# Putting parts of the split weights 64 bytes further on in SBUF, so that the starts of a matmul's moving operand and of the next matmul's weights fall in chosen halves of 128 bytes

## The chip, the cores and the metric

The kernel runs on one core of a Trainium2 chip. The metric is the device time of one launch in microseconds (us); the table below gives three runs of the kernel before.

## The reference

A four-part encoder trunk over 256 tokens of width 1024, in float32: a layer with neighbourhood attention and latent attention side by side, an MLP, a layer of dilated attention, a second MLP, and RMS norms between them. Cut to the parts whose weights the change touches:

```python
def sq_relu_mlp(xn, w1, w2):
    return jnp.square(jax.nn.relu(xn @ w1)) @ w2

def odd_mixer(xn, w_in, w_o, cos_f, sin_f):
    b, s, _ = xn.shape
    hcat = (xn @ w_in).reshape(b, s, DIL_GROUPS, 3, DIL_HEADS, HEAD_DIM)
    q = apply_rope(hcat[:, :, :, 0], cos_f, sin_f)
    k = apply_rope(hcat[:, :, :, 1], cos_f, sin_f)
    v = hcat[:, :, :, 2]
    return dilated_attention(q, k, v) @ w_o

for layer in range(DEPTH):                     # DEPTH = 2
    xn = rms_norm(x, norm_mix[layer])
    ...                                        # even_mixer, then odd_mixer
    x = x + sq_relu_mlp(rms_norm(x, norm_mlp[layer]), mlp_w1[layer], mlp_w2[layer])
return rms_norm(x, norm_final)
```

## The kernel before, in words

**Split operands.** Every product is made of float32r matmuls on operands that are split in two: a high part (`hi`, a cast on ScalarE, line 201) and a low part (`lo`, the difference, on VectorE, line 202). Most products take three matmuls (`mm3`, lines 205 to 207): high weights by high, high by low, low by high. Two products pack the first two into one of 512 columns, because high and low parts of the activations lie side by side in the tile `pair` (`[P, 8, 2, 256]`): the MLP's up projection (line 391: high weights by 512 columns of `pair`; line 394: low weights by its 256 high columns) and the odd layer's queries and keys (lines 911 and 914, the same way).

**Weights.** They come from HBM in blocks of up to 2048 columns into four `raw` buffers (`load_weight`, line 163) and are split in four pieces each (`split_piece`, line 178) into the tiles `whi` and `wlo` of the pool `wsp`, three buffers each, one block ahead of use (`weight`, line 192). The list `specs` (lines 131 to 158) fixes the order of the blocks. The very first blocks are split by hand in the even layer (lines 593 to 628), where `views` (line 594) makes the tiles.

**Which operand is which.** A matmul has a stationary operand, loaded by an instruction of its own (LDWEIGHTS, on the profile's PEld), and a moving one that streams past it. TensorE's weight load for the next matmul runs while the present one streams. The block's weights are stationary in the up projections (`w1`), the odd layer's queries and keys (`w_oqk`), and the even layer's queries and keys and both output projections. They are the moving operand, with the activations stationary, in the values (`w_v` of the even layer, `w_ov` of the odd one: 512 columns, stationary `pair`), the latent parts, and the down projections (`w2`: 512 columns, stationary `hh` and `hl`).

**Order.** In an MLP, each step makes the next 256 features (32 matmuls of lines 391 and 394) and folds in the features of three steps before (24 matmuls of lines 205 to 207). In the odd layer the blocks of `w_oqk` and `w_ov` are woven with the attention of the unit before (`ODD_PLAN`, `weave`).

**Where the tiles lie.** In the program as built (byte addresses within a partition): `pair` begins at 26944, which is 64 past a multiple of 128, in the second half of 128 bytes. The three `whi` begin at 121216, 129408 and 137600 and the three `wlo` at 145792, 153984 and 162176, all at multiples of 128 (and 384 past a multiple of 2048), in the first half. `hh` and `hl` also begin in the first half, the mixed heads `oah`, `oal`, `obh` and `obl` in the second. Nearly every slice that a matmul takes starts a multiple of 128 bytes into its tile, so the half of the tile is the half of the operand.

Of the kernel before, what the change touches and what calls it, by code (L numbers as in the profile page):

```python
# [17 lines left out]
F32R = mybir.dt.float32r  # L18
# [5 lines left out]
P = 128  # L24
# [10 lines left out]
WCH = 2048  # L35
# [3 lines left out]
SPLIT_AHEAD = 2  # L39
WPARTS = 4  # L40
NORM_PRIO = 300

QK_ORDER = (0, 2, 1)


def odd_weights():


    v = lambda b, c: [("w_ov", b, c, h) for h in range(2)]
    qk = lambda u, js=QK_ORDER: [("w_oqk", u, j) for j in js]  # L50
    out = [p for pair in zip(v(0, 0), v(0, 1)) for p in pair] + qk(0)
    for step in ODD_PLAN:
        for kind, *at in step:
            out += v(*at) if kind == "v" else qk(*at)
    return out
# [13 lines left out]
def trunk(ctx, tc, a, out):  # L69
# [6 lines left out]
    wsp = ctx.enter_context(tc.tile_pool(name="wsp", bufs=WBUFS))  # L76
    ps = ctx.enter_context(tc.tile_pool(name="ps", bufs=4, space=PSUM))

    def scratch(shape, name):

        n = int(np.prod(shape))
        v = work.tile([P, 512], F32, tag="scratch", name=name, bufs=12)[:, :n]
        if len(shape) == 2:
            v = v.rearrange("p (a b) -> p a b", b=shape[1])
        return v
# [45 lines left out]
    specs = []  # L131

    def plan(name, n):
        for j in range(a[name].shape[0]):
            specs.append((a[name][j], n))

    def plan_mlp(layer):
        for j in (0, 1):
            specs.append((a["w1"][layer, j], WCH))
        for j in range(2, 16):  # L140
            specs.append((a["w1"][layer, j], WCH))
            specs.append((a["w2"][layer, j - 2], WCH))
        for j in (14, 15):
            specs.append((a["w2"][layer, j], WCH))

    CV = 416 + 512
    plan("w_cv", 2 * CV)
# [5 lines left out]
    plan("w_oe", 2 * D)  # L153
    plan_mlp(0)
    for kind, *at in odd_weights():
        specs.append((a[kind][tuple(at)], WCH))
    plan("w_oo", 2 * D)
    plan_mlp(1)

    parts = {}  # L160
    state = {"loaded": 0, "split": 0, "used": 0}

    def load_weight(edges=None, earlier=lambda i: None):
        j = state["loaded"]
        src, n = specs[j]
        raw = wraw.tile([P, WCH], F32, tag="raw", name="raw")
        edges = edges or (0, n)
        for i, c in enumerate(slice(*e) for e in zip(edges, edges[1:])):
            earlier(i)
            nc.sync.dma_start(raw[:, c], src[:, c])  # L170
        parts[j] = [raw, None, None]
        state["loaded"] = j + 1

    def cut(j, i, n):
        w = specs[j][1] // n
        return slice(i * w, (i + 1) * w)

    def split_piece(eng=None):
        j, i = divmod(state["split"], WPARTS)
        if i == 0:  # L180
            parts[j][1:] = (wsp.tile([P, WCH], F32R, tag=n, name=n) for n in ("whi", "wlo"))
        raw, hi, lo = (z[:, cut(j, i, WPARTS)] for z in parts[j])
        state["split"] += 1
        return split(hi, lo, raw, eng)
# [15 lines left out]
    def split(hi, lo, src, eng=None):  # L200
        a = nc.scalar.copy(hi, src).ins  # L201
        return a, (eng or nc.vector).tensor_tensor(lo, src, hi.bitcast(F32), op=ALU.subtract).ins  # L202
# [35 lines left out]
    def prepare(k, n, xT):  # L238

        hi, lo, gk = xT[0][:, k, :], xT[1][:, k, :], gains[:, n * KT + k:n * KT + k + 1]  # L240
        return (lambda: nc.scalar.activation(hi, x[:, k, :], AF.Copy, scale=gk),
                lambda: nc.vector.scalar_tensor_tensor(lo, x[:, k, :], gk, hi.bitcast(F32), ALU.mult, ALU.subtract))  # L242
# [21 lines left out]
    def rstd(s):  # L264

        r = work.tile([P, NT], F32, tag="rstd", name="rstd")
        nc.gpsimd.tensor_tensor(r, columns(s), mhalf.broadcast_to([P, NT]), op=ALU.pow)
        return r
# [19 lines left out]
    def column(r, t):  # L288
        return r[:, t:t + 1]
# [8 lines left out]
    def join(b, o, n, xT):  # L298

        v = x[:, 2 * b:2 * b + 2, :]  # L300
        nc.vector.tensor_tensor(v, two(o), v, op=ALU.add)
        for f in zip(*(prepare(k, n, xT) for k in (2 * b, 2 * b + 1))):
            run_all(f)

    def hand_over(accs, last, n):

        xT, s = pair_tile(), sum_tile()
        for b in range(4):
            last[b]()
            with tc.high_priority(NORM_PRIO):  # L310
                join(b, accs[b], n, xT)
        return xT, s

    def hand_over_tokens(accs, last, n, scale):
# [4 lines left out]
        def leave(h, t):  # L319
            last(h, t)  # L320
            acc, sc = accs[2 * t + h], column(scale, t)
            with tc.high_priority(NORM_PRIO):
                y = ys[h, t] = scratch([512], "y")
# [3 lines left out]
        def turn(h):  # L327
            with tc.high_priority(NORM_PRIO):
                for b in range(2):
                    pt = bank("w")  # L330
                    for k in range(2):
                        for t in range(NT):
                            c = (2 * b + k) * P
                            nc.tensor.transpose(pt[:, k * T + t * P:k * T + (t + 1) * P], ys[h, t][:, c:c + P], ident)
                    join(2 * h + b, pt, n, xT)
# [181 lines left out]
    def even(ep):  # L517
# [36 lines left out]
        def product(o, n, w, k, t, passes=range(3)):  # L554

            xs = xh[:, k, tok(t)], xl[:, k, tok(t)], xh[:, k, tok(t)]
            for i in passes:
                nc.tensor.matmul(o[:, 0:n], xs[i], (w[1], w[1], w[2])[i], start=(k, i) == (0, 0), stop=(k, i) == (KT - 1, 2))  # L558
# [26 lines left out]
        def v_out(t, pv):  # L585
            nc.scalar.activation(vna[:, t, :], pv, AF.Copy, scale=column(r, t))
# [6 lines left out]
        with tc.manual_schedule(engines={ENG.PE, ENG.Activation, ENG.DVE}):  # L593
            def views(j, c0, c1):
                if parts[j][1] is None:
                    parts[j][1:] = (wsp.tile([P, WCH], F32R, tag=n, name=n) for n in ("whi", "wlo"))
                return [z[:, c0:c1] for z in parts[j]]

            for k in range(KT):
                upper, lower = prepare(k, 0, xT)  # L600
                upper()
                if k < 4:
                    c0 = k % 2 * CV
                    wc, wv = views(k // 2, c0, c0 + 416), views(k // 2, c0 + 416, c0 + CV)
                else:
                    wc, wv = views(2, (k - 4) * 416, (k - 3) * 416), None
                if k == 0:

                    nc.vector.tensor_copy(wc[1], wc[0])
                    lower()  # L610
                    nc.vector.tensor_tensor(wc[2], wc[0], wc[1].bitcast(F32), op=ALU.subtract)
                else:
                    lower()
                    split(wc[1], wc[2], wc[0])
                if wv:
                    split(wv[1], wv[2], wv[0])

                if k in (3, 5, 6, 7):
                    squares.pop(0)()
                for w, ps_, n in ((wc, pc, 416), (wv, pv, 512)):  # L620
                    if w is not None:
                        for passes in ((0,), (1,), (2,)) if k == 0 else (range(3),):
                            for t in range(NT):
                                product(ps_[t], n, w, k, t, passes)
            state["split"] = 3 * WPARTS
            for i in range(2 * WPARTS):
                split_piece()
            wv = [z.rearrange("p (k n) -> p k n", k=4) for z in parts[3]]
            for t in range(NT):
                for k in range(4, KT):  # L630
                    product(pv[t], 512, [z[:, k - 4] for z in wv], k, t)
                    if (t, k) == (0, 5):
                        r = rstd(s)
            rs = work.tile([P, 2, NT], F32, tag="rs", name="rs", bufs=1)
            for i, n in enumerate((256, 128)):
                nc.vector.tensor_scalar(rs[:, i, :], r, n ** -0.5, None, ALU.mult)
            dg = [diagonal(r, t) for t in range(NT)]
            turn_c = [c_tail(t, pc[t]) for t in range(NT)]
            state["used"] = 4
            for j in range(4):  # L640
                del parts[j]
            for t in range(NT):
                v_out(t, pv[t])
# [176 lines left out]
        at = -5  # L820
# [11 lines left out]
    def odd(op, xT, s):  # L832
# [22 lines left out]

        def value_steps(b, c, prio=NORM_PRIO, tag="acc"):

# [39 lines left out]
        def qk_steps(d, js=QK_ORDER):  # L897
# [4 lines left out]
            def gemm(b, f, half):  # L902
# [12 lines left out]
                if half == 1:  # L915
                    with tc.high_priority(NORM_PRIO):
                        if f == 0:
# [48 lines left out]
        def attention(u, d):  # L966
# [36 lines left out]
            def mix(out_tag):  # L1003
                pvo = bank(out_tag)
                v0, v12 = values_of(u)
                for i in range(NT):
# [4 lines left out]
                    for c in range(2):  # L1011
                        qs = slice(64 * c, 64 * c + 64)
                        for j in range(2):
                            cs = slice(64 * j, 64 * j + 64)
                            nc.tensor.matmul(pvo[cs, i * P + 64 * c:i * P + 64 * c + 64], v12[:, 2 * i + c, cs], turned[i, j][:, 2, qs], start=False, stop=c == 1)
                with tc.high_priority(NORM_PRIO):
                    split(*(z[:, u % 4, :] for z in mixed[u // 4]), pvo[:, 0:T])
# [152 lines left out]
```

## Time and profile before

| what | value |
|---|---|
| median of three runs | 742.25 us (741.9 to 743.02) |
| the profiled execution's own time | 742.68 us |
| its span in the profile | 740.9 us |
| granted TensorE clock | 0.998 of full |
| PE busy | 732.5 us, 99% of the span, 4539 matmuls |
| VectorE busy | 538.6 us, 73% |
| ScalarE busy | 471.4 us, 64% |
| DMA | 180 GB/s mean |

The profile records when each matmul starts and how long it takes. Matmuls overlap: the next one starts before the one before has drained. So there are two ways to read what one costs: the distance from one start to the next (its gap), and its recorded duration, which is longer than the gap by about the same amount for all of one width. A group's row in the list of one source line gives the count and the shortest, median and longest duration in ns.

### The profile page before, as it was taken

How to read it: one execution, taken by the hardware profiler on the slowest of the kernel's cores; microseconds unless marked ns; L12 is line 12 of the kernel's file. 1: busy time of each engine (PE TensorE's matmuls, PEld its weight loads, DVE VectorE, ACT ScalarE, POOL GpSimd, SP SyncE). 2: the span in 40 equal slices, each digit the busy share in tenths (PEclk: the TensorE clock that was granted, in tenths of full speed). 3: DMA queues.
4: the chain of work that ended last, by engine and by line, in shares of the span. 5: the costliest groups of instructions: out<-in, count | busy, mean ns of one | idle time of the engine just before them, and what ended most of it. 6: DMA issues, size and time to landing. Idle time of an engine off the chain costs nothing.

```text
span 740.9 us, 11984 instructions
## 1 busy us (share of the span) xinstructions
PE 732.5 (99%) x4539; PEld 628.5 (85%) x4539; DVE 538.6 (73%) x1100; ACT 471.4 (64%) x1020; POOL 8.4 (1%) x20
## 2 busy tenths in 40 slices
PE   9999999999999999999999999999999999999996
PEld 6988998888888887888888888888898888888885
DVE  6878859766665666689968886899559765665674
ACT  7788967554455456468877668687857455455441
POOL 0100000000000001000000000000000000000000
PEclk9999999999999999999999999999999999999999
DMA  8773335565555554655664545455546555545501
GB/s 291 313 263 108 115 114 177 175 218 174 197 197 178 202 188 155 232 160 171 208 220 147 221 145 182 139 192 173 188 152 220 178 175 197 197 171 189 206 4 57
DMA packets 24585, 133.17 MB, mean 180 GB/s; under 512 B 3664, under 2 KB 4816, under 8 KB 10192
## 3 DMA queue, kind: packets, MB, share of 16 engines
q1 hardware_dynamic: 24384, 132.28, 52.0%
q8 instruction: 35, 0.57, 0.3%
q14 instruction: 22, 0.18, 0.1%
q10 hardware_dynamic: 144, 0.13, 0.1%
HBM read 127.16 MB, written 1.05 MB: 173 GB/s over the span
## 4 chain that ended last, share of the span: by engine, by line
PE 94%; DMA 1%; DVE 1%; issue 1%; ACT 1%; SPq 1%; POOLq 0%; POOL 0%
PE w L391 16%; PE acc L205 13%; PE acc L207 13%; PE acc L206 13%; PE acc L911 11%; PE w L394 8%; PE acc L914 5%; PE acc L558 2%; PE w L214 1%; PE w L999 1%; PE w L205 1%; PE w L768 1%; PE w L207 1%; PE w L206 1%; PE w L979 1%
## 5 line engine op out<-in xcount | busy, mean ns | idle before, releaser
L202 DVE TENSOR_TENSOR wlo<-raw,whi 128x512 fp32r<-128x512 f32 (+2 forms) x471 | 303.0, 679 | 68.2 <-ACT whi L201 67.6
L201 ACT CAST whi<-raw 128x512 fp32r<-128x512 f32 (+2 forms) x471 | 261.9, 614 | 140.5 <-PE acc L207 57.0
L391 PE MATMUL w<-pair,whi 128*128 128x512 f32 x512 | 125.0, 395 | 0.0
L391 PEld LDWEIGHTS w<-pair,whi 128*128 128x128 f32 x512 | 95.2, 187 | 22.9 <-DVE pair L242 0.6
L911 PE MATMUL acc<-pair,whi 128*128 128x512 f32 x384 | 101.6, 401 | 0.0
L205 PE MATMUL acc<-whi,hh 128*128 128x512 f32 x250 | 97.9, 392 | 0.0
L207 PE MATMUL acc<-whi,hl 128*128 128x512 f32 x250 | 97.7, 391 | 0.0
L206 PE MATMUL acc<-wlo,hh 128*128 128x512 f32 x250 | 97.6, 390 | 0.0
L911 PEld LDWEIGHTS acc<-pair,whi 128*128 128x128 f32 x384 | 67.7, 188 | 12.4 <-issue 0.2
L398 DVE TENSOR_TENSOR u<-w,side 128x256 f32<-128x256 f32 x64 | 26.9, 421 | 57.2 <-ACT side L397 57.1
L394 PEld LDWEIGHTS w<-pair,wlo 128*128 128x128 f32 x512 | 63.4, 188 | 2.9
L394 PE MATMUL w<-pair,wlo 128*128 128x256 f32 x512 | 63.9, 277 | 0.0
L201 ACT CAST hh<-hsq 128x512 fp32r<-128x512 f32 x32 | 19.9, 622 | 56.4 <-DVE hsq L400 56.4
L207 PEld LDWEIGHTS acc<-whi,hl 128*128 128x128 f32 x250 | 47.0, 188 | 9.7
L914 PEld LDWEIGHTS acc<-pair,wlo 128*128 128x128 f32 x384 | 51.2, 188 | 4.4
L205 PEld LDWEIGHTS acc<-whi,hh 128*128 128x128 f32 x250 | 47.0, 188 | 8.7
L206 PEld LDWEIGHTS acc<-wlo,hh 128*128 128x128 f32 x250 | 46.9, 188 | 8.8
L914 PE MATMUL acc<-pair,wlo 128*128 128x256 f32 x384 | 51.9, 278 | 0.0
L205 PE MATMUL acc<-whi,pair 128*128 128x512 f32 x80 | 32.3, 403 | 0.0
L207 PE MATMUL acc<-whi,pair 128*128 128x512 f32 x80 | 31.5, 393 | 0.0
L206 PE MATMUL acc<-wlo,pair 128*128 128x512 f32 x80 | 31.2, 390 | 0.0
L990 ACT ACTIVATE pp<-sn,dmn 128x384 f32<-128x384 f32 x32 | 19.7, 614 | 9.8 <-DVE dmn L988 8.9
(220 smaller groups left out, 1102.4 us busy)
## 6 DMA issues: line engine op xcount, KB each, us to landing
raw<-in_w SPq DMA_DIRECT2D x64, 1024.0 KB, 4.8
raw<-in_w_oqk SPq DMA_DIRECT2D x24, 1024.0 KB, 4.9
raw<-in_w_ov SPq DMA_DIRECT2D x12, 1024.0 KB, 5.0
raw<-in_w_qk SPq DMA_DIRECT2D x4, 1024.0 KB, 8.6
raw<-in_w_oe SPq DMA_DIRECT2D x4, 1024.0 KB, 5.3
sw<-qk SPq DMA_DIRECT2D x64, 64.0 KB, 2.0
raw<-in_w_oo SPq DMA_DIRECT2D x4, 1024.0 KB, 5.3
bias<-in_rpb SPq DMA_DIRECT2D x8, 256.0 KB, 4.6
```

The costliest lines, as they stand in the source:

```text
L201: a = nc.scalar.copy(hi, src).ins
L202: return a, (eng or nc.vector).tensor_tensor(lo, src, hi.bitcast(F32), op=ALU.subtract).ins
L205: nc.tensor.matmul(o, sh, mh, start=first, stop=False)
L206: nc.tensor.matmul(o, sh, ml, start=False, stop=False)
L207: nc.tensor.matmul(o, sl, mh, start=False, stop=last)
L391: nc.tensor.matmul(two(pu[f]), w[0][:, cut_of(k, f)], xT[2][:, k], start=k == 0, stop=False)
L394: nc.tensor.matmul(pu[f][:, 0:T], w[1][:, cut_of(k, f)], xT[0][:, k, :], start=False, stop=k == KT - 1)
L398: nc.vector.tensor_tensor(u[:, f], pu[f][:, 0:T], side[:, f], op=ALU.add)
L558: nc.tensor.matmul(o[:, 0:n], xs[i], (w[1], w[1], w[2])[i], start=(k, i) == (0, 0), stop=(k, i) == (KT - 1, 2))
L911: nc.tensor.matmul(two(pq), wh[:, cut_of(k)], xp[:, k], start=k == 0, stop=False)
L914: nc.tensor.matmul(pq[:, 0:T], wl[:, cut_of(k)], xh[:, k, :], start=False, stop=k == KT - 1)
L990: nc.scalar.activation(pp, sn, AF.Exp, bias=mn, scale=-1.0, accum_out=z)
```

## The change

The tiles `whi` and `wlo` grow from 2048 to 2080 columns (by 128 bytes), and of each the 2048 columns that begin either at its start or 16 columns (64 bytes) in are used. `SHIFTS` says which: the high part of `w1` and of `w_oqk` is put off by 64 bytes and the low part is not; both parts of `w_v` and `w_ov` are put off; all other weights stay at the start of their tiles.

As the tiles are longer, the later buffers also move: in the program as built the three `whi` tiles begin at 121216, 129536 and 137856 and the three `wlo` at 146176, 154496 and 162816. These are still multiples of 128, but 384, 512 and 640 (and 768, 896 and 1024) past a multiple of 2048. All other tiles keep their half of 128 bytes. The instructions of every engine, their order and their waits stay the same.

```diff
+LINE = 16
+SHIFTS = {"w1": (LINE, 0), "w_oqk": (LINE, 0), "w_ov": (LINE, LINE), "w_v": (LINE, LINE)}
+
...
     def plan(name, n):
         for j in range(a[name].shape[0]):
-            specs.append((a[name][j], n))
+            specs.append((a[name][j], n, SHIFTS.get(name, (0, 0))))
 
     def plan_mlp(layer):
         for j in (0, 1):
-            specs.append((a["w1"][layer, j], WCH))
+            specs.append((a["w1"][layer, j], WCH, SHIFTS["w1"]))
...
     for kind, *at in odd_weights():
-        specs.append((a[kind][tuple(at)], WCH))
+        specs.append((a[kind][tuple(at)], WCH, SHIFTS[kind]))
...
+    def split_tiles(j):
+        return [wsp.tile([P, WCH + 2 * LINE], F32R, tag=n, name=n)[:, o:o + WCH] for n, o in zip(("whi", "wlo"), specs[j][2])]
+
...
     def split_piece(eng=None):
         j, i = divmod(state["split"], WPARTS)
         if i == 0:
-            parts[j][1:] = (wsp.tile([P, WCH], F32R, tag=n, name=n) for n in ("whi", "wlo"))
+            parts[j][1:] = split_tiles(j)
...
             def views(j, c0, c1):
                 if parts[j][1] is None:
-                    parts[j][1:] = (wsp.tile([P, WCH], F32R, tag=n, name=n) for n in ("whi", "wlo"))
+                    parts[j][1:] = split_tiles(j)
```

More of the change, by code (lines that the diff above doesn't have):

```diff
@@ L134, in plan @@
         for j in range(a[name].shape[0]):
-            specs.append((a[name][j], n))
+            specs.append((a[name][j], n, SHIFTS.get(name, (0, 0))))
     def plan_mlp(layer):
         for j in (0, 1):
-            specs.append((a["w1"][layer, j], WCH))
+            specs.append((a["w1"][layer, j], WCH, SHIFTS["w1"]))
         for j in range(2, 16):
-            specs.append((a["w1"][layer, j], WCH))
-            specs.append((a["w2"][layer, j - 2], WCH))
+            specs.append((a["w1"][layer, j], WCH, SHIFTS["w1"]))
+            specs.append((a["w2"][layer, j - 2], WCH, (0, 0)))
         for j in (14, 15):
-            specs.append((a["w2"][layer, j], WCH))
+            specs.append((a["w2"][layer, j], WCH, (0, 0)))
     CV = 416 + 512
@@ L164, in load_weight @@
         j = state["loaded"]
-        src, n = specs[j]
+        src, n, _ = specs[j]
         raw = wraw.tile([P, WCH], F32, tag="raw", name="raw")
```

## Prediction

> **What bounds the kernel now.** I read the page first, for the engine that fills the span, and the chain of waits that ended last.
>
> ```profile
> span 740.9 us, 11984 instructions
> PE 732.5 (99%) x4539; PEld 628.5 (85%) x4539; DVE 538.6 (73%) x1100; ACT 471.4 (64%) x1020; POOL 8.4 (1%) x20
> PEclk9999999999999999999999999999999999999999
> PE 94%; DMA 1%; DVE 1%; issue 1%; ACT 1%; SPq 1%; POOLq 0%; POOL 0%
> ```
>
> PE is busy for 99% of the span, the clock is full in every slice, and 94% of the closing chain is PE. The waits of PE alone say whether anything feeds it late:
>
> ```profile
> PE acc L117 <- DVE warm L112: 1.2, 1, 1.2
> PE w L979 <- DVE q L940: 0.7, 1, 0.7
> PE acc L205 <- DVE obl L202: 0.2, 1, 0.2
> ```
>
> These three rows are all there is, 2.1 us together. So the time is a sum of gaps between matmul starts, and a matmul that starts its successor 1 ns earlier 1,000 times takes 1 us off the end. An edit that leaves instructions, order and waits alone can act only on those gaps (or on the splitting engines, below). The question is whether the gap depends on where operands begin. Next I read the list by source line of every large group of 512 columns; the three figures are shortest, median and longest duration in ns.
>
> ```profile
> L391 PE MATMUL w<-pair,whi x512: 388/394/497, 113.5 to 715.9; 128*128 128x512 f32 x171
> L911 PE MATMUL acc<-pair,whi x384: 388/394/504, 315.3 to 513.1; 128*128 128x512 f32 x192
> L205 PE MATMUL acc<-whi,hh x250: 387/389/484, 130.3 to 729.5; 128*128 128x512 f32 x125
> L206 PE MATMUL acc<-wlo,hh x250: 387/389/481, 130.5 to 729.8; 128*128 128x512 f32 x125
> L207 PE MATMUL acc<-whi,hl x250: 387/389/478, 130.8 to 730.0; 128*128 128x512 f32 x125
> L205 PE MATMUL acc<-whi,pair x80: 388/394/481, 292.1 to 525.6; 128*128 128x512 f32 x80
> L206 PE MATMUL acc<-wlo,pair x80: 388/388/398, 292.3 to 525.8; 128*128 128x512 f32 x80
> L207 PE MATMUL acc<-whi,pair x80: 391/392/400, 292.5 to 526.0; 128*128 128x512 f32 x80
> ```
>
> All are 128x128 weights by 512 columns, and yet they have two medians. Against the built program's addresses the difference has a pattern. In the down projections (hh, hl) the moving operand and the weights loaded beside it for the next matmul both begin in the first half of 128 bytes: 389. In the up projection and in the odd layer's queries and keys (L391, L911) pair moves from the second half while the next weights come from the first: 394. The values (whi or wlo moving, pair stationary) have different halves too, and lie between, 388 to 394. At 256 columns the sign turns round:
>
> ```profile
> L394 PE MATMUL w<-pair,wlo x512: 276/276/283, 117.9 to 717.8; 128*128 128x256 f32 x171
> L914 PE MATMUL acc<-pair,wlo x384: 276/276/287, 317.2 to 514.1; 128*128 128x256 f32 x192
> L205 PE MATMUL w<-whi,hh x12: 277/283/283, 730.2 to 734.2; 128*128 128x256 f32 x12
> L206 PE MATMUL w<-wlo,hh x12: 282/283/283, 730.3 to 734.3; 128*128 128x256 f32 x12
> L914 PE MATMUL acc<-pair,wlo x6: 276/276/283, 405.2 to 405.8; 128*128 128x256 f32 x6
> ```
>
> Different halves (L394, L914) take 276, the same half (hh at 256 columns, in the tail) 283. The last row is the best test that the trace has: it is the end of one run of eight, of which the last is followed by a transpose whose weights begin in pair's own half. That last one is the 283; its neighbours, with the same line, shape and moving tile, are 276. Over the span ten matmuls of L914 are followed so, and each takes 280 to 283.
>
> **What a gap is worth.** Durations end by a model, so I take the price from starts, in the timeline of one MLP step (start, length, line, operands):
>
> ```profile
> 153.06 0.39 PE L205 MATMUL acc<-whi,hh 128*128 128x512 f32 x1
> ...
> 158.51 3.89 PE L391 MATMUL w<-pair,whi 128*128 128x512 f32 x16
> 162.25 1.99 PE L394 MATMUL w<-pair,wlo 128*128 128x256 f32 x16
> ```
>
> From 153.06 to 158.51 stand 24 matmuls of the down projection: 5.45 / 24 = 227.1 ns each. From 158.51 to 162.25 stand 16 of L391: 3.74 / 16 = 233.8 ns. The starts give 6.7 ns, the medians 394 - 389 = 5; I take 6 for L391. For the odd layer the chain has runs of eight:
>
> ```profile
> 349.31 1.87 PE acc L911 x8
> 361.62 2.06 PE acc L911 x8
> 364.59 1.86 PE acc L911 x8
> ```
>
> 1.87 / 8 = 233.8 in quiet runs; 2.06 holds a stall of about 0.19 us that the halves don't touch. In the trace's starts these gaps alternate between about 231 and 236, and the first of a run is often 226, so I take 5 there.
>
> **The change part by part.** Nothing is added or removed, no DMA, queue or wait moves. The counts are of pairs (a matmul and the one behind it on PE), from the addresses of both built programs.
>
> - High part of w1, 64 bytes on: 480 of L391's 512 pairs go from different halves to the same. 480 x 6 = 2.9 us gained. The other 32 stand before L394, whose low weights stay in the first half: unchanged.
> - High part of w_oqk: 324 pairs of L911, 324 x 5 = 1.6 us.
> - Both parts of w_ov, the moving operand: 284 pairs in thirds. To 389 from 394 (L205), 388 (L206) and 392 (L207) is 5, -1 and 3, a mean of 2.3: 284 x 2.3 = 0.65 us.
> - Both parts of w_v in the even layer: 23 pairs of L558, by the same mean 0.05 us.
> - What is lost: 29 pairs of 512 columns go from same to different (24 of them the last down matmul before the next L391), 29 x 6 = 0.17 us; 38 of 256 columns go from different to same (low weights ahead of a shifted high part), 38 x 7 by the 283 and the 276 = 0.27 us.
>
> The sum is 2.9 + 1.6 + 0.65 + 0.05 - 0.17 - 0.27 = 4.8 us gained. The low products L394 and L914, 896 matmuls, keep different halves, which is the cheaper case at 256 columns; the down projections keep the same half, the cheaper one at 512.
>
> ScalarE and VectorE now write the shifted tiles from 64 bytes on. The trace has no such write of this shape, only the aligned ones:
>
> ```profile
> L202 DVE TENSOR_TENSOR wlo<-raw,whi 128x512 fp32r<-128x512 f32 x456 | 295.5, 684 | 66.6 <-ACT whi L201 66.0
> L201 ACT CAST whi<-raw 128x512 fp32r<-128x512 f32 x456 | 255.1, 618 | 138.7 <-PE acc L207 57.0 <-issue 55.5 <-PE acc L911 8.7
> 310.00:550.00 240.00, 239.18 (x1713) 208.28 (x1712) 192.39 (x393) 178.14 (x377) 0.69 (x1) 1.00 0.54 179
> ```
>
> The window of the odd layer (columns PE, PEld, VectorE, ScalarE) shows the tightest place: VectorE is busy for 192 of 240 us there. A few per cent on 684 ns would stay hidden beside PE; the faster PE leaves it 240 - 2.3 us, still 80% busy. I cost the writes at nothing. If each took a quarter longer (171 ns), a third of the 456, some 150, falling here would add 26 us, VectorE would reach 218 of 238 us and its peaks would begin to hold PE up, so this decides only from about there.
>
> On the profiled execution's footing the time is 742.68 - 4.8 = 737.9. That execution was 0.43 above the median of the runs, so against the median it is 742.25 - 4.8 = 737.4 us.
>
> **Bounds.** Taking 6.7 for all of L391 and L911 gives 5.4, and 388 for the values (6, 0, 4) 284 x 3.3 = 0.9: with the losses 5.9, so 736.4. Taking 4 for L391, 3 for L911 and nothing for the values gives 1.9 + 1.0 - 0.4 = 2.5, so 739.8. The forecast's own range is 736 to 740.
>
> **Rivals.**
>
> *The operands' starts don't matter.* The 389 and the 394 would then belong to the products: another moving tile, another PSUM tile, other work on VectorE beside them. The time would stay 742.3. For it speaks that L206 on pair has 388 with different halves. Against it speaks the 283 at the end of a run of 276, where only the next weights differ (in type too, which is its weakness), and the three hh rows at 256. The Trainium skill, in "SBUF — State Buffer", section "SBUF: two separate sides", has it that TensorE, ScalarE and VectorE's own pair of ports never wait for anyone, so that two reads by TensorE could not meet; by that rule the gain is nothing and the time 742.3. No run here has yet set it against a shifted tile; the 283 beside 276 speaks against it. Chance 0.13, with the case that the shift doesn't do what it says.
>
> *The distance matters over 256 bytes, not 128: slower.* The longer tiles put whi and wlo 128 bytes apart from each other in their place modulo 256. Now 331 pairs of the down projections go from a distance of 0 to 128, and 330, 217 and 157 of the gaining pairs of L391, L911 and the values arrive at 128 and not at 0. The trace of before has no pair of 512 columns at 128. If 128 costs c ns more than 0, the change is worth 331c + 330(c - 6) + 217(c - 5) + 157(c - 2.3) ns, with the pairs that do reach 0 worth -1.7 us and the losses 0.4 us: 1.035c - 4.8 us. It is slower from c = 4.6; with c = 6, the price that 64 has, the time is 742.25 + 1.4 = 743.7. Of the 256-column pairs 783 move from a distance of 64 to 192 as well; at up to 7 ns each they would add up to 5.5, so 749 at the worst. For it speaks that the values, at 192, cost 388 to 394 and not 394 throughout; against, that within L391 and within the down projections one value rules. I give it 0.10.
>
> *The moving operand alone decides.* A stream from the second half would be slow at 512 columns whatever the weights do. L391 and L911 stay at 394, and the values, now moving from the second half, rise from 388 to 394 to 394 throughout: 284 x 2.7 = 0.8 us, so 743.0. The values' present place between 388 and 394 speaks for it, the 283 after the 276 against. Chance 0.05.
>
> *The shifted writes slow the splits* so far that VectorE holds PE up in the odd layer, above: a time over 743. Chance 0.02.
>
> **How the numbers follow.** The forecast has 0.70, the rivals 0.13, 0.10, 0.05 and 0.02. About 0.2%, 1.5 us, is what a measurement of this kernel can tell from no change, so faster means below 740.8 and slower above 743.7. The forecast is faster in nearly all of its range, and I give 0.02 of the period rival (c well below 4.6) to it: 0.72. Same gets the first rival, most of the moving-operand one and some of the period one: 0.19. Slower gets the rest, 0.09. The range must take in the unchanged time to leave no more than 2 in 10 outside: 736.0 to 742.8.
>
> **What would show it.** In the profile after, the medians of L391 and L911 (seven lines further down) fall from 394 to about 389, with 388 to 389 for all three rows of the values; the hh rows stay at 389, and the low products at 276. If L391 has two values by buffer, or hh rises to 394 for some, the period rival is right; if 394 stays, one of the other two. The splits stay near 684 and 618. I am wrong if the gaps fall and the span doesn't, because then PE isn't what the time is made of.

## The result, and the profile after

The changed kernel takes 746.16 us (median of 6 runs, 746.04 to 746.78) against 742.28 (6 runs, 741.89 to 743.02): a ratio of 1.0052, 95% interval 1.0039 to 1.0065. It is slower by 3.9 us where 4.8 us of gain were forecast. The profiled execution took 746.22 us, 3.5 more than that of before.

The page of the changed kernel and its waits of PE say that the bound is the same: PE fills the span, and what it waits for is less than before (1.4 us, not 2.1).

```profile
span 744.4 us, 11984 instructions
PE 736.7 (99%) x4539; PEld 631.1 (85%) x4539; DVE 540.4 (73%) x1100; ACT 471.5 (63%) x1020; POOL 8.3 (1%) x20
PE 96%; ACT 1%; issue 1%; DVE 1%; DMA 1%; SPq 0%; POOLq 0%; POOL 0%
```

```profile
PE acc L121 <- DVE warm L116: 1.2, 1, 1.2
PE acc L212 <- DVE obl L209: 0.2, 1, 0.2
```

So the time came into the gaps. The list by source line of the changed kernel (lines stand seven further down; shortest, median and longest duration in ns):

```profile
L398 PE MATMUL w<-pair,whi x512: 387/393/504, 113.5 to 719.3; 128*128 128x512 f32 x171
L918 PE MATMUL acc<-pair,whi x384: 387/393/502, 317.1 to 515.0; 128*128 128x512 f32 x192
L212 PE MATMUL acc<-whi,hh x250: 388/397/483, 130.3 to 733.1; 128*128 128x512 f32 x125
L213 PE MATMUL acc<-wlo,hh x250: 387/395/476, 130.5 to 733.4; 128*128 128x512 f32 x125
L214 PE MATMUL acc<-whi,hl x250: 387/392/477, 130.7 to 733.6; 128*128 128x512 f32 x125
L401 PE MATMUL w<-pair,wlo x512: 276/280/285, 117.9 to 721.3; 128*128 128x256 f32 x171
L921 PE MATMUL acc<-pair,wlo x384: 276/280/285, 319.0 to 516.0; 128*128 128x256 f32 x192
```

Three things are to be seen. The up products and the odd layer's queries and keys (L398, L918), which were to fall from 394 to 389, are at 393. The down projections, which no shift touches, went from 389 to 397, 395 and 392. The low products, untouched as well, went from 276 to 280. The timeline shows the same step as in the prediction:

```profile
153.09 0.39 PE L212 MATMUL acc<-whi,hh 128*128 128x512 f32 x1
...
158.69 3.88 PE L398 MATMUL w<-pair,whi 128*128 128x512 f32 x16
162.41 0.28 PE L401 MATMUL w<-pair,wlo 128*128 128x256 f32 x1
```

24 down matmuls take 5.60 us, 233.3 ns each (227.1 before); 16 up matmuls 3.72 us, 232.5 each (233.8 before). The splits stayed where they were:

```profile
L209 DVE TENSOR_TENSOR wlo<-raw,whi 128x512 fp32r<-128x512 f32 x456 | 295.6, 684 | 68.6 <-ACT whi L208 67.8
L208 ACT CAST whi<-raw 128x512 fp32r<-128x512 f32 x456 | 255.1, 618 | 140.7 <-PE acc L214 59.8 <-issue 55.0 <-PE acc L918 10.1
```

As the order of the matmuls is the same, each gap from one recorded start to the next can be set against the same gap of before. Summed by kind, in us, with the kernels of the experiments beside it (each one's profiled execution against that of before):

| kernel | up | queries, keys | low, MLP | low, odd layer | down | values | rest | sum |
|---|---|---|---|---|---|---|---|---|
| forecast | -2.9 | -1.6 | 0 | 0.3 | 0.2 | -0.7 | | -4.8 |
| the change | -0.9 | -0.5 | +1.5 | +1.0 | +2.8 | +0.4 | -0.7 | +3.6 |
| e2 | -0.7 | -0.4 | +1.0 | +0.9 | +2.8 | +0.5 | -0.2 | +3.8 |
| e3 | -0.4 | -0.2 | -0.3 | +0.5 | 0.0 | 0.0 | -0.8 | -1.2 |
| e4 | -2.8 | -0.8 | +1.6 | +0.8 | +0.6 | 0.0 | -0.2 | -0.8 |
| e5 | 0.0 | 0.0 | -0.1 | 0.0 | 0.0 | 0.0 | -0.8 | -0.9 |
| e6 | -0.1 | -0.1 | +1.6 | +1.2 | +0.5 | +0.1 | -0.4 | +2.8 |
| e7 | -2.8 | 0.0 | +1.6 | 0.0 | +0.6 | 0.0 | -0.4 | -1.0 |
| e9 | -2.5 | 0.0 | -0.5 | 0.0 | 0.0 | 0.0 | +0.6 | -2.4 |
| e10 | -1.4 | -0.6 | +0.1 | +0.6 | +0.1 | 0.0 | -1.0 | -2.2 |
| e11 | -2.5 | -0.6 | -0.5 | +0.6 | 0.0 | 0.0 | -0.1 | -3.2 |

The rest is start-up and the attention's short waits; it differs by 0.8 us in e5, which changes no distance at all, so a sum is only as good as that, while the other columns of e5 differ by at most 0.1.

### The profile page after: what moved, and what is told of

It is laid out like the page before. It is cut to its first block, busy times and chain, and to the rows that moved or that the text cites. A ratio compares the mean times of both kernels' runs of the same rounds, so it can differ in the third digit from the quotient of the medians.

```text
span 744.4 us, 11984 instructions
## 1 busy us (share of the span) xinstructions
PE 736.7 (99%) x4539; PEld 631.1 (85%) x4539; DVE 540.4 (73%) x1100; ACT 471.5 (63%) x1020; POOL 8.3 (1%) x20
## 4 chain that ended last, share of the span: by engine, by line
PE 96%; ACT 1%; issue 1%; DVE 1%; DMA 1%; SPq 0%; POOLq 0%; POOL 0%
PE w L398 16%; PE acc L212 13%; PE acc L213 13%; PE acc L214 13%; PE acc L918 12%; PE w L401 8%; PE acc L921 6%; PE acc L565 3%; PE w L1006 1%; PE w L221 1%; PE w L212 1%; PE w L214 1%; PE w L213 1%; PE w L775 1%; PE w L986 1%
## 5 line engine op out<-in xcount | busy, mean ns | idle before, releaser
L398 PE MATMUL w<-pair,whi 128*128 128x512 f32 x512 | 124.2, 394 | 0.0
L398 PEld LDWEIGHTS w<-pair,whi 128*128 128x128 f32 x512 | 95.4, 188 | 22.2 <-DVE pair L249 0.8
L918 PE MATMUL acc<-pair,whi 128*128 128x512 f32 x384 | 101.2, 400 | 0.0
L918 PEld LDWEIGHTS acc<-pair,whi 128*128 128x128 f32 x384 | 67.8, 188 | 12.1 <-issue 0.2
L401 PE MATMUL w<-pair,wlo 128*128 128x256 f32 x512 | 65.4, 280 | 0.0
L995 DVE CUSTOM_DVE_ANT_0 sn<-w,mask 128x384 f32<-128x384 f32 x32 | 17.5, 547 | 11.2 <-PE w L986 11.2
```

The costliest lines, as they stand in the source:

```text
L398: nc.tensor.matmul(two(pu[f]), w[0][:, cut_of(k, f)], xT[2][:, k], start=k == 0, stop=False)
L401: nc.tensor.matmul(pu[f][:, 0:T], w[1][:, cut_of(k, f)], xT[0][:, k, :], start=False, stop=k == KT - 1)
L918: nc.tensor.matmul(two(pq), wh[:, cut_of(k)], xp[:, k], start=k == 0, stop=False)
L995: nc.vector.tensor_tensor_reduce(out=sn, in0=ss[j][:, 0:384], in1=mask[:, i, :], op0=ALU.add, op1=ALU.min, scale=-(HD ** -0.5), scalar=3e3 ...
```

## The experiments

Two questions stood open: what slowed the down and the low products, and why the shifted ones gained so little. The theories were the two of the prediction, halves of 128 bytes and a period of 256 bytes.

### e1: the gaps by themselves

```diff
+        for n in NAMES:                 # letters a to h: weights 0, 64, ... 448 bytes past the moving operand
+            group("wide", n, 512, 24)
+        for n in NAMES:
+            group("woff", n, 512, 24, move=1)      # both 64 bytes further on
+        for n in NAMES:
+            group("afterb", "b", 512)
+            group("lowb", n, 256)
+        for n in NAMES:
+            group("aftera", "a", 512)
+            group("lowa", n, 256)
```

> This kernel leaves the whole computation out: it only runs groups of 16 or 24 matmuls (128x128 float32r weights) in which the next weights begin 0, 64, ... 448 bytes (letters a to h) past the moving operand, modulo 512. Its time is of no interest, only the gaps in its trace. Theory of the record (halves of 128): in the 512-column groups wide and woff the letters a, c, e, g have 227 ns and b, d, f, h 233; at 256 columns (lowa, lowb) a, c, e, g 120 and b, d, f, h 114. Period of 256: only a and e have 227 at 512 columns, and c and g about 233 as b does. Entry: low runs always the same distance (b) at 256 columns after different 512-column groups; if the gap is a matter of addresses alone all eight have 114, if it depends on what ran before they fall into 113 to 114 after b, d, f, h and 118 after a. The tri groups copy the down projection with the second moving tile 0 or 128 bytes off and the weights 0 or 128 off: 227 for triaa, 229 to 233 for trica and tricc.

The rows of the list by tile for the 512-column groups, and for 256 columns behind a group at distance 64 (lowb) and behind one at 0 (lowa):

```profile
L50 PE MATMUL wide<-mv,sta x24: 388/389/389, 37.3 to 42.5; 128*128 128x512 f32 x24
L50 PE MATMUL wide<-mv,stb x24: 390/396/398, 42.8 to 48.1; 128*128 128x512 f32 x24
L50 PE MATMUL wide<-mv,stc x24: 390/392/404, 48.4 to 53.7; 128*128 128x512 f32 x24
L50 PE MATMUL wide<-mv,std x24: 388/392/398, 53.9 to 59.2; 128*128 128x512 f32 x24
L50 PE MATMUL wide<-mv,ste x24: 388/389/395, 59.5 to 64.7; 128*128 128x512 f32 x24
L50 PE MATMUL lowb<-mv,stb x16: 276/276/281, 135.2 to 136.9; 128*128 128x256 f32 x16
L50 PE MATMUL lowb<-mv,stc x16: 279/281/285, 140.8 to 142.6; 128*128 128x256 f32 x16
L50 PE MATMUL lowb<-mv,std x16: 277/279/284, 146.4 to 148.2; 128*128 128x256 f32 x16
L50 PE MATMUL lowa<-mv,stb x16: 280/281/283, 179.9 to 181.7; 128*128 128x256 f32 x16
```

Letters a and e agree, and c does not agree with them: the period is 256 bytes. (The letters go in steps of 64 bytes; finer distances were not tried.) In gaps between starts (mean of the last twelve of a group), 512 columns take 226.7 ns at a distance of 0, 233.3 at 64, 231.7 at 128 and 228.9 at 192, and the next four letters repeat it. The woff groups, with both operands 64 bytes further on, give the same four numbers, so it is the distance and not the place of either. At 256 columns, behind a group at 64, the best is 64, with 113.3; 128 takes 118.4 and 192 takes 117.8, 0 from 119 to 120. And the last row shows what no theory of the prediction had, and what the entry groups were made to ask: the same addresses at 256 columns take 113.3 ns behind a group at 64 but 117.8 behind a group at 0, for the whole run of 16. A run falls into one of two rhythms at its start and keeps it. Of the eight letters ahead only b and f gave 113.3; behind d and h, for which 113 to 114 had been expected too, the runs take 117.8.

The Trainium skill, "SBUF — State Buffer", section "SBUF: two separate sides", has TensorE never waiting on anyone. Here matmuls of equal shape, with no other engine at work beside them, start 6.6 ns further apart (233.3 and 226.7) by where the weights begin against the moving operand, so the measurement decides against the rule as the prediction applied it. What makes the difference inside the chip the runs do not show.

### e2: the longer tiles alone

```diff
-SHIFTS = {"w1": (LINE, 0), "w_oqk": (LINE, 0), "w_ov": (LINE, LINE), "w_v": (LINE, LINE)}
+SHIFTS = {"w1": (0, 0), "w_oqk": (0, 0), "w_ov": (0, 0), "w_v": (0, 0)}
```

> The longer tiles alone (2080 columns, so the buffers move by multiples of 128), nothing put off. Period of 256: the down projections, whose distances become 0 or 128, take what they take in the changed kernel (medians 397, 395, 392 and not 389), about 2.9 us more in all; the up products stay at 394 and the low ones at 276; time about 745.2. Halves of 128 (the moved buffers don't matter): everything as before, 742.3. If the shift and not the moved buffers made the change slower, also 742.3.

Measured: 746.68 us, ratio 1.0056 (1.0043 to 1.0068), 1.5 us above the 745.2 expected by the period of 256. Without any shift the whole slowdown is there.

```profile
L212 PE MATMUL acc<-whi,hh x250: 388/397/483, 130.7 to 733.4; 128*128 128x512 f32 x125
L213 PE MATMUL acc<-wlo,hh x250: 387/394/482, 130.9 to 733.7; 128*128 128x512 f32 x125
L214 PE MATMUL acc<-whi,hl x250: 388/392/479, 131.2 to 733.9; 128*128 128x512 f32 x125
L401 PE MATMUL w<-pair,wlo x512: 276/279/285, 118.4 to 721.5; 128*128 128x256 f32 x171
```

The down projections do what the period's expectation said, 2.8 us. The low products rise as well, which it did not say (it had them at 276): in two of three buffers their distance went from 64 to 192, which e1 prices at 118.

### e3, e4 and e5: the shift without moving the buffers

These use high tiles 256 bytes longer and low tiles as before, so that nothing moves modulo 256; memory is too short to do that for both parts. e3 puts the high parts of w1 and w_oqk off by 64 bytes (distance 128), e4 by 192 (distance 0), e5 not at all; in the lines below k stands for these three amounts.

```diff
+SHIFTS = {"w1": (k * LINE, 0), "w_oqk": (k * LINE, 0), ...}        # k = 1 in e3, 3 in e4, 0 in e5; values 0
...
+        hi = wsp.tile([P, WCH + 4 * LINE], F32R, tag="whi", name="whi")
+        return [hi[:, specs[j][2][0]:specs[j][2][0] + WCH], wsp.tile([P, WCH], F32R, tag="wlo", name="wlo")]
```

> High part of w1 and w_oqk put off by 64 bytes as in the change, but in tiles that are 256 bytes longer and only for the high part, so that no buffer moves modulo 256: the distance to pair is 128 in all buffers, the down projections are where they were. Halves of 128: up products and the odd layer's queries and keys fall from 394 to 389, time 737.5 to 739.8. Period of 256: they alternate between about 229 and 238 ns (median 232 to 233), no gain, 742 to 743, and 745 if the low products go to 118 ns as in the changed kernel.

> As e3_keep128, but put off by 192 bytes: the distance to pair is 0 modulo 256 in all buffers. Period of 256: up products and the odd layer's queries and keys fall to 388 (227 ns), 804 x 6 = 4.8 us gained; the low products at 256 columns, if they go to 118 ns behind such groups, give 2.9 back: 740.4, else 737.5. Halves of 128: the same time as e3_keep128. If the entry doesn't matter, the low products stay at 276.

> The control to e3 and e4: tiles of the high parts 256 bytes longer, nothing put off, so every distance modulo 256 is that of before. Period of 256: as before, 742.3, with 394, 389 and 276 for up, down and low products. If any move of the buffers costs (a longer period, as 512 or 2048), the down projections rise as in e2, to 744 or more.

Measured: e3 741.79 us (ratio 0.9993, 0.9984 to 1.0002), e4 741.91 (0.9993, 0.9984 to 1.0002), e5 742.25 (0.9998, 0.9989 to 1.0007). None is told apart from before, but they get there in different ways. e3, then e4:

```profile
L213 PE MATMUL acc<-whi,hh x250: 387/389/482, 129.9 to 728.3; 128*128 128x512 f32 x125
L399 PE MATMUL w<-pair,whi x512: 387/393/505, 113.2 to 714.7; 128*128 128x512 f32 x171
L402 PE MATMUL w<-pair,wlo x512: 276/276/283, 117.6 to 716.6; 128*128 128x256 f32 x171
```

```profile
L399 PE MATMUL w<-pair,whi x512: 387/389/504, 113.9 to 715.0; 128*128 128x512 f32 x171
L402 PE MATMUL w<-pair,wlo x512: 276/281/287, 118.2 to 717.0; 128*128 128x256 f32 x171
```

In e3 the down projections are back at 389, and the shift of the change, in its purest form, gains almost nothing on the up products (393, and 0.4 us of the 2.9 forecast): same half, but 128 bytes apart. With e1's letters a and c, that refutes the halves; the time is 0.2 us under the 742 to 743 of the period. In e4, at a distance of 0, the up products do fall to 389, 2.8 us; but the low products, whose addresses are untouched, go from 276 to 281 and give 2.4 us back, and 0.6 more is lost where the down projections start behind them. e4 was expected at 740.4 for this case, 1.5 less than measured: the odd layer's runs of eight gained 0.8 us where 1.9 (324 x 6 ns) were counted, and the 0.6 was not foreseen.

### e6: the low products' distance alone

```diff
+SHIFTS = {"w1": (0, 2 * LINE), "w_oqk": (0, 2 * LINE), "w_ov": (0, 0), "w_v": (0, 0)}
...
+        lo = wsp.tile([P, WCH + 4 * LINE], F32R, tag="wlo", name="wlo")
```

> Only the low parts of w1 and w_oqk put off, by 128 bytes, with the low tiles 256 bytes longer: the low products' distance to pair goes from 64 to 192, all else keeps its distance. Halves of 128: no change, 742.3. Period of 256: the low products go from 113 or 114 to 118 ns (medians 276 to 280), 896 x 4 = 3.6 us, and the groups behind them may start in another rhythm: 745.5 to 746.5.

Measured: 745.11 us, ratio 1.0038 (1.0026 to 1.0051); a little under the range.

```profile
L402 PE MATMUL w<-pair,wlo x512: 277/279/284, 118.3 to 720.6; 128*128 128x256 f32 x171
L922 PE MATMUL acc<-pair,wlo x384: 276/280/285, 318.6 to 516.0; 128*128 128x256 f32 x192
```

64 and 192 begin in the same half of 128 bytes, and still the low products lose 2.8 us (1.6 and 1.2). This is the second way to see the period, and it prices what the moved buffers did to the low products in e2.

### e7 and e8: what sets the rhythm

e7 is e4 with the distance of 0 for w1 alone (the lines are against e4):

```diff
-SHIFTS = {"w1": (3 * LINE, 0), "w_oqk": (3 * LINE, 0), "w_ov": (0, 0), "w_v": (0, 0)}
+SHIFTS = {"w1": (3 * LINE, 0), "w_oqk": (0, 0), "w_ov": (0, 0), "w_v": (0, 0)}
```

> As e4, but only the high part of w1 put off by 192 bytes (distance 0), w_oqk not. If the runs of 8 in the odd layer lost by their starts what they gained, this is better than e4: up products 2.6 us less, low products of the MLPs 1.6 us more, 741.0 to 741.5. Halves of 128: 738.5 to 739.5. If the low products' rhythm is set by the operands' addresses alone and not by the group ahead, they stay at 276 and the time is 739.3.

Measured: 741.67 us, ratio 0.9991 (0.9982 to 1.0000), just over what was expected: up products -2.8, low ones +1.6, down +0.6.

e8 repeats whole MLP steps of matmuls, with all pairs of letters and with the last one to four of the 16 matmuls of 512 columns changed:

```diff
+        for x in "abcd":
+            for y in "abcd":
+                step(x + y, x * 16, y * 16)
+        for n in (1, 2, 3, 4):
+            step("m" + "wxyz"[n - 1], "a" * (16 - n) + "b" * n, "b" * 16)
```

> This kernel leaves the whole computation out. It repeats MLP steps of matmuls alone (16 of 512 columns with letter x of the distance, 16 of 256 columns with letter y, 24 in the pattern of the down projection at distance 0; a, b, c, d are 0, 64, 128, 192 bytes). If distance modulo 256 and the rhythm left by the group ahead are the whole story, the step bb (before) takes 16 x 233.3 + 16 x 113.3 + 24 x 226.7 = 11.0 us plus its starts, ab some 35 ns less (low products at 118), aa 16 x 2.2 ns more than ab, and cd, with the down projection's tiles 128 off, about 0.2 us more than bb. The steps mw to mz end the 512-column group with 1 to 4 matmuls at distance 64: if these few set the rhythm, the low products go back to 113 and the step is 70 ns shorter than ab; if a longer run is needed they stay at 118. By halves of 128 alone, a and c agree, and b and d.

The low products (l, then the step's name) in the list by tile, at the same addresses in all four, with the groups mw, mx and my ending in one, two and three matmuls at distance 64:

```profile
L52 PE MATMUL lab<-mv,stb x48: 280/281/283, 61.8 to 85.5; 128*128 128x256 f32 x48
L52 PE MATMUL lmw<-mv,stb x48: 276/276/281, 559.1 to 582.6; 128*128 128x256 f32 x48
L52 PE MATMUL lmx<-mv,stb x48: 280/281/283, 591.8 to 615.6; 128*128 128x256 f32 x48
L52 PE MATMUL lmy<-mv,stb x48: 276/276/281, 624.8 to 648.4; 128*128 128x256 f32 x48
```

One or three set the good rhythm, two or four do not. The gaps between the recorded starts (ns, one step each) show what goes with it:

```
ab  512 columns, last four: 227 227 226 226   256 columns: 118 118 117 118 118 118 117 119 ...
mw  512 columns, last four: 227 227 226 235   256 columns: 119 113 113 114 113 113 114 113 ...
mx  512 columns, last four: 226 226 236 231   256 columns: 118 118 117 118 118 118 117 118 ...
my  512 columns, last four: 225 236 231 236   256 columns: 118 114 113 113 114 113 113 114 ...
```

At distance 64 long gaps (236) and short ones (231) take turns, and in these steps a run of 256 columns behind a long gap falls into 113, behind a short one or behind 227 into 118. In the kernel before it is the same: all 69 runs behind a gap of 233 or more are in the good rhythm, all 11 behind 231 or less in the other. The last gap is not the whole of it, though. In e8's step pe, whose 16 matmuls go six at 0, two at 64, and the same again, the last gap is 235 and the run behind takes 118 in all three repeats; behind e1's letters d and h it is 237 or 238, and the run takes 117.8. What else decides was not found. The step mw takes 10.92 us against 10.98 for ab and 11.09 for bb, whose 512-column group ended here on the short gap; with its low products in the good rhythm bb would be at about 11.02 (an estimate, 16 x 4.4 ns less). The expected steps held for ab and mw; bb with 113 was not, by the turn.

### e9, e10 and e11: arrangements by the new rule

e9 moves the last 128 columns of each block of w1 by another 64 bytes, so that only the last of the 16 up matmuls has distance 64. The cast and the difference of that piece are each done in two, 64 instructions more in all. e10 needs no trick: distance 192 for the high parts of w1 and w_oqk. e11 takes e9 for w1 and e10 for w_oqk. The lines of `SHIFTS` are again against e4.

```diff
+        off = 4 * LINE if self.off == 3 * LINE and c0 >= LAST else self.off         # LAST = 2048 - 128
+        return self.z[rows, c0 + off:c1 + off]
...
-SHIFTS = {"w1": (3 * LINE, 0), "w_oqk": (3 * LINE, 0), "w_ov": (0, 0), "w_v": (0, 0)}
+SHIFTS = {"w1": (3 * LINE, 0), "w_oqk": (0, 0), "w_ov": (0, 0), "w_v": (0, 0)}        # e9
+SHIFTS = {"w1": (2 * LINE, 0), "w_oqk": (2 * LINE, 0), "w_ov": (0, 0), "w_v": (0, 0)}  # e10
```

> As e7 (high part of w1 at distance 0), but the last 128 columns of each block of w1 64 bytes further on, so that of the 16 matmuls ahead of the low products the last one has distance 64 and the 15 others 0. By e8's steps mw and ab this one matmul puts the low products back into the rhythm of 113 ns: up products about 2.5 us less than before, low products as before (276 again), 739.3 to 739.8. If the low products' rhythm has another source, they stay at 118 ns and the time is that of e7, 741.7. By halves of 128, the same as e7.

> As e4, but the high parts of w1 and w_oqk put off by 128 bytes, to a distance of 192 from pair. By e8's steps the up products take 229.3 ns (step db) with the low products at 113.7, no trick needed: 480 x 4 = 1.9 us less in the MLPs, up to 0.6 less in the odd layer, 739.8 to 740.5. If they fall into the other rhythm that e1 showed at this distance (233.3), 742.3. By halves of 128 this changes nothing: 742.3.

> e9 for w1 and e10 for w_oqk together, the cheapest arrangement by the period of 256 that fits the memory: if the two add up, 0.3 to 0.6 us less than e9, 738.8 to 739.4. If the odd layer's short runs of 8 lose at their starts what they gain, the same as e9.

Measured: e9 739.76 us, ratio 0.9962 (0.9949 to 0.9974); e10 740.79, 0.9981 (0.9972 to 0.9990); e11 739.43, 0.9959 (0.9946 to 0.9971). All three beat both kernels. e9:

```profile
L421 PE MATMUL w<-pair,whi x512: 387/389/503, 114.7 to 713.5; 128*128 128x512 f32 x171
L424 PE MATMUL w<-pair,wlo x512: 276/276/282, 119.0 to 715.4; 128*128 128x256 f32 x171
```

The up products stay at 389, as in e7, and the low ones are back at 276: one matmul's 64 bytes in each step return the 1.6 us that e7 had lost, and the 0.6 of the down projections. e10 is 0.3 us over its range:

```profile
L399 PE MATMUL w<-pair,whi x512: 388/394/502, 113.2 to 713.7; 128*128 128x512 f32 x171
L402 PE MATMUL w<-pair,wlo x512: 276/276/284, 117.6 to 715.6; 128*128 128x256 f32 x171
L922 PE MATMUL acc<-pair,wlo x384: 276/281/287, 316.2 to 512.4; 128*128 128x256 f32 x192
```

The mean gap of its up products is 230.4 ns, between e1's two rhythms at this distance (228.9 and 233.3), and in the odd layer the low products lose the 0.6 us that the queries and keys gain. For the same reason e11, at the upper edge of its range, is not told apart from e9: its 0.6 us on the queries and keys goes to the odd layer's low products.

## Why the prediction was wrong

**Right.** PE bounds the kernel and a gap saved reaches the end: the sum of the gaps, +3.6 us, is the change of the profiled time, +3.5. The gap depends on where operands begin, and the pairs of before had the signs that were read off: 389 against 394, 276 against 283. The writes at 64 bytes cost nothing (684 and 618 before and after).

**Wrong: "The low products L394 and L914, 896 matmuls, keep different halves, which is the cheaper case at 256 columns; the down projections keep the same half, the cheaper one at 512."** This is the step that failed. It took the half of 128 bytes to be what decides. In the kernel before distances of 0 and 64 bytes modulo 256, and 192 for the values, are all that occurs at 512 columns, so its trace could not tell a period of 128 from one of 256. The longer tiles brought 128 (and 192 for the low products), and e2 shows that alone they cost the whole of it. The down projections took +2.8 us, the low products +2.5, of which a part by their distance (e6) and a part by the rhythm left by the group ahead (e4, e7: the same addresses, 281 and not 276).

**Wrong by the same step: the gain of 2.9 us on w1 and 1.6 on w_oqk.** Two buffers of three arrive at a distance of 128, which e3 shows to be worth 0.4 and 0.2 us when all are there. They gained 0.9 and 0.5. The values, 0.65 forecast as a gain, lost 0.4.

**The rival that was right, with its terms.** A period of 256 bytes had 0.10 and its price at c = 6 was 743.7, the worst case with the low products 749; the time lies between them. Its two mechanisms were the two that happened, but its sum was not: with the 5.0 ns that e1 measured between 128 and 0 (231.7 and 226.7) it gives 742.25 + 1.035 x 5.0 - 4.8 = 742.6. The rest came from the low products, 2.5 us, and from the down projections, 2.8 us where 331 pairs at 5.0 ns make 1.7. What it lacked was the rhythm. The weight that was given to it was too small for what the profile had: the values, at 192, did not fit two halves, and that row was noted and passed over.

**Still open.** The cost of a mixed pattern does not follow from the four numbers of e1. In the changed kernel the down projections repeat 236, 234, 230 in two buffer sets and 232, 226, 229 in the third, and e1's patterns with the same distances (trica, tricc) gave 228.8 for both. e8 has the first of these patterns again, in its steps xs, xu and xv: there it took about 231 in seven repeats and about 233.3 in the two others, both of xv, with the 235 or 236, 234 or 235 and 230 of the changed kernel. So one set of distances has at least three rhythms at 512 columns, and which one a run takes was seen, not derived.

## What to carry to other kernels

When a bound is the distance between matmul starts, a few ns each are decided by the distance between the moving operand's and the weights' addresses, modulo 256 bytes here (seen in steps of 64), and by the run that went before; measure the gap over all distances, in a small kernel, before a rule is drawn from the few that a trace happens to hold. An edit that lengthens a tile moves every buffer behind it: make a control that lengthens and does nothing else. And count what the untouched neighbours do, since here the gain on one group was given back by the next.

## What the runs showed that was not expected

- A run of equal matmuls keeps one of two rhythms for its whole length: at 256 columns and distance 64, 113.3 or 117.8 ns (e1, e8). In the kernel before 69 of 80 runs of low products were in the first, in the changed one 10 of 80, counted by the median gap of each run.
- The prediction counted pairs of a moving operand and the next matmul's weights, but a gap does not hang on that pair alone. In e8 mw the last of the 16 has weights at 64; the gap ahead of it, in which those weights were loaded, stays at 226, and the one behind it is 235. The weights loaded in that one lie at 64 too, but in ab, where they do while the last matmul's own lie at 0, the gap is 226. The next weights do count elsewhere: with the last matmul's own at 0 and the next at 128 (ac) the gap is 232 or 233.
- Longer tiles and moved buffers cost nothing by themselves: e5, with all distances modulo 256 kept, is at 742.25 us against 742.5 of before on its chip. Writes at 64 bytes past a tile's start cost nothing either (684 and 618 ns, as before).
